# A hybrid SSD and attention layer: the issue orders of the engines rewritten from the state sums to the last output tiles

## The chip, the cores and the metric

One core of a Trainium2 chip runs the whole program. The time is the device time of one execution in microseconds, lower is better. TensorE is called PE, VectorE DVE, ScalarE ACT, GpSimd POOL and SyncE SP, as in the profile.

## The reference

One layer of a streaming encoder, for a prompt of 512 frames and for the next 64 frames of a running stream. D_MODEL is 1024; there are 8 SSD heads of 64 with a state of 128, and 8 latent attention heads.

```python
h = rmsnorm(x, norm_mix); proj = h @ w_in           # z, xbc, dt_raw, cq, ckv_raw
xbc, conv_new = causal_conv(xbc, conv_buf, conv_w, conv_b)   # 4 taps, silu -> xs, B, C
dt = softplus(dt_raw + dt_bias); A = -exp(a_log)
y, h_new = ssd_scan(xs, dt, A, B, C, ssm_h0)        # chunks: per chunk
    # cum = cumsum(dt*A); decay = exp(cum_l - cum_s), causal
    # y = (decay * (C.B) * dt) . x + exp(cum) * (C . h)
    # h = exp(cum_last) * h + (exp(cum_last - cum) * dt * x) . B
y_ssd = rmsnorm((y + d_skip * xs) * silu(z), ssd_norm)
q = rmsnorm(cq) @ w_uq; c_kv = rmsnorm(ckv); q_rope, k_rope rotated
o = mla_attend(...)      # softmax(q.k, block causal) . keys_c, then @ w_uv
x = x + concat(y_ssd, o) @ w_out
hf = rmsnorm(x, norm_ffn)
x = x + (silu(hf @ w_gate) * (hf @ w_up)) @ w_down  # D_FF = 2816
y = rmsnorm(x, norm_final)
```

Outputs are y for both groups, the new latent keys, the new SSD states and the last three convolution rows.

## The kernel before

The 512 + 64 = 576 columns of both groups run together, in two halves of 288. Channels lie on the 128 partitions. Large products keep float32 accuracy by splitting each operand into a high and a low part of type fp32r: `split_weights` (lines 123 to 129) has ACT cast a raw weight tile wr to wh (L127) and DVE subtract to get wl (L128), and each product is three matmuls, wh with x high, wh with x low, wl with x high. `product_halves` (L455) does that for one half of 288 columns in one PSUM bank and then calls an evacuation.

The stages that matter here, in order of time:

- Convolution tiles, `conv_tile` (L394): DVE adds three taps into cacc, ACT takes a tanh, cth (L410), and DVE multiplies into xs (xsd) or into B and C (bc, L412 for the prompt, L413 for the 64 sample columns). Tile 7 is the last of them; its two DVE steps need cth7.
- z tiles, `z_tile` (L471): ps_z on PE, DVE's evacuation into zh (L476), ACT's tanh zt (L479), DVE's product sz.
- SSD by chunks of 128 columns, chunks 0 to 3 for the prompt and chunk 4 for the 64 sample columns. `chunk_a` (L490) has SP load the cumulative sums from DRAM: cumb, and ecp in two halves (L502); PE transposes xs (ps_x) and B (ps_b, L514) and multiplies B with C (ps_b, L515). `chunk_e` (L520) forms the decays E by exponentials on ACT (L529) and the exponential of ecp (L530). `chunk_b` (L543) makes the outputs ps_y and the part from the state, ps_i (L561); `chunk_s` (L565) the state sum ps_s and the new state h. `gate` multiplies with silu(z).
- Attention by head pairs: `pair_proj` (L618) makes ps_q and ps_k, copied to qs and ks; `scores` (L673) makes sc and sc_s (L686), `soft` (L656) takes the max (mx) on DVE, the exponential pr with its sum on ACT (L664), and scales pr by 1/sum on DVE for the first head (L670) and on ACT for the second (L668). `turn` (L692) transposes pr on PE into ptp (L702) and copies it to pt, by ACT for the first head and DVE for the second (L704); `turn_s` is the same for the sample columns (ptp_s, L710). `values` multiplies with V (pv, L727), `values_s` likewise (pvs, L738).
- cat_y: DVE scales xs by the norm factor Ry (L775), ACT casts the high part (L157), DVE subtracts the low part (L159).
- Output projection, `out_tile` (L746): ps_o (L465), added to the residual x2 by DVE (L758); o0 uses the SSD half of w_out and cat_y, o1 the attention half as well.
- Feed-forward, from about 242 us to the end, two thirds of the span.

The code lists the steps in two strings (ORDER_SSD, ORDER_ATT) that fix which instructions exist. The order in which each engine takes its instructions is another matter: at the very end `issue_in_order` reads one table for each engine, ISSUE, a list of positions among the instructions made for that engine, and ties each to the one ahead of it. So each engine's list is fixed by hand, and semaphores only make it wait.

```python
def issue_in_order(tc, nc):
    engines = {"PE": nc.tensor, "DVE": nc.vector, "ACT": nc.scalar, "POOL": nc.gpsimd, "SP": nc.sync}
    info = mybir.DependencyInfo(mybir.DependencyClass.NoSync, mybir.DependencyReason.DATA)
    for name, text in ISSUE.items():
        made = [i for i in nc.cur_bb.bb.instructions if i.engine == engines[name].engine]
        order = list(_places(text))
        for a, b in zip(order, order[1:]):
            tc.add_manual_dep(made[b], made[a].name, info, reason="issue order")
```

A second table, PLACES, fixes the buffer that each temporary, weight tile and PSUM bank takes. It stays.

Of the kernel before, what the change touches and what calls it, by code (L numbers as in the profile page):

```python
# [1319 lines left out]
602-612 637 641-644 638-640 657-659 665-688 660 689-736 661-662 737-760 771-794 663-664 645-652 763-766 653-656  # L1320
795-818 767-770 761-762 819-826 859-861 833-836 862-864 827-832 865-866 837-839 867 880-883 840 868-870 841 845-852
871-873 853-856 874-879 842-843 904-906 857-858 884-887 907-909 844 888 910-912 892-903 889-891 913-915 925-934
916-921 935 939-940 922-924 936-938 949-957 964-965 941 966 945-948 967-969 942-944 970-971 958-963 972-974 976-979
975 987-988 980 984-985 1003 991-993 981-983 986 1015 1004-1006 989 994-995 1016-1021 996 1007-1014 1022-1026
1029-1034 997 1043-1045 990 1000-1002 998-999 1046-1054 1035-1042 1027-1028 1059-1060 1055 1075-1092 1056-1058
1093-1104 1121-1123 1065-1067 1124 1061-1062 1071-1072 1063-1064 1130-1132 1068-1070 1125-1129 1073 1133-1156
1105-1108 1074 1229-1237 1119-1120 1238 1241 1239-1240 1242-1252 1157 1111-1114 1109-1110 1253-1264 1158 1176
1265-1276 1115-1118 1159-1161 1177-1179 1162-1175 1277-1285 1289-1290 1180-1183 1188-1189 1184-1187 1205-1206
1190-1192 1227 1193-1198 1291-1297 1199-1201 1228 1202-1204 1286-1288 1215-1220 1207-1214 1221 1318 1222-1224 1298
1225-1226 1299-1306 1319 1307 1320 1308-1317 1321-1322 1330-1332 1323 1342-1343 1348-1351 1344-1345 1352-1354 1346  # L1330
1355 1347 1333 1324-1329 1334-1341 1356-1363 1368 1364-1366 1369-1370 1367 1371-1393 1404 1394-1396 1405-1406
1397-1403 1407-1415 1428 1416-1427 1429-1433 1440-1441 1434-1435 1442 1436-1439 1572 1443-1447 1452 1448 1453-1456
1449 1457-1458 1450 1459-1460 1451 1461-1462 1587 1578 1584 1463 1581 1573 1464-1478 1579 1479-1486 1575 1488 1487
1489 1585 1490-1497 1500 1498 1501-1503 1499 1586 1588 1504-1506 1576 1574 1507 1580 1508-1509 1512 1577 1513 1510
1514-1515 1511 1516-1517 1605 1518-1522 1593 1523-1525 1582-1583 1526-1527 1606 1528-1531 1602 1536 1532 1537 1533
1538 1534 1603 1539 1607 1535 1589 1540-1541 1599 1542-1544 1594 1608 1545-1550 1600 1551-1552 1595 1614 1553-1555
1609 1560 1556-1557 1626 1561-1565 1615 1558-1559 1566-1568 1616 1569-1570 1604 1571 1596 1590 1597-1598 1601 1591
1610 1617 1620 1623 1621 1635 1627 1622 1592 1636 1629 1637 1628 1611 1641 1618 1630 1624 1631 1612-1613 1625
1658-1659 1642 1644 1650 1660 1647 1661-1662 1632-1633 1663 1651 1648 1664-1665 1619 1656 1638-1640 1666 1643 1667
1634 1668 1645 1669 1646 1649 1652-1654 1657 1694 1670-1672 1695-1697 1673 1682 1698 1655 1674 1699 1675 1700 1718  # L1340
# [12 lines left out]
1988-1989 2042 2013 1990 2043 2055 2006 2056 2014-2015 1991 2007 2001 2044 2048 1992-1993 2057 2002 2058-2059 1984
2008-2009 2045 2016 2003-2005 1985-1986 2017 2049 2046-2047 1994 1987 1995 2010 1996 2011 2018 1997 2060-2061 2019
2062 2020-2021 2030 2063 2022 2031 2064 2023 2065-2066 2050 2067-2069 1998 2032 2070 2051-2052 1999 2053 2033
2071-2073 2034 2074-2075 2084-2086 2076 2078 2035 2077 2079 2036 2087 2080-2081 2037 2088 2082 2114 2083 2102 2090
2089 2038 2091 2103 2039-2040 2115 2092 2041 2093 2104 2094 2105 2095 2106 2096 2107 2116-2118 2138 2097-2099 2139
2108 2100 2109 2101 2119 2110 2192 2111-2112 2120 2113 2121 2126 2122 2127 2123 2128-2130 2140 2131 2144 2132 2145
2193 2133 2124 2134 2146-2148 2135 2149-2150 2136 2194 2137 2141 2125 2142 2195-2196 2151 2143 2197 2156 2152-2153
2157-2158 2154 2159 2168 2160-2162 2180 2155 2163 2181 2169 2164-2165 2182 2174 2222 2170-2171 2216 2166 2210 2175  # L1360
2172 2183 2173 2167 2184 2223 2217 2176 2211 2177 2224 2186 2212 2225 2187-2188 2218 2178-2179 2219 2213-2215 2185
2189-2190 2226 2191 2234 2198 2220 2199-2200 2235 2228-2230 2221 2204 2231-2232 2236 2201 2237-2239 2233 2227
2205-2206 2240 2202 2246 2241 2203 2242 2252 2243-2245 2207 2247 2253-2254 2248 2270 2255 2208 2282 2256-2258 2283
2259-2260 2271-2272 2261 2284 2262-2264 2273 2285 2209 2265 2286 2266 2274 2267 2275 2268 2287 2269 2288-2289 2276
2290 2277 2249 2306 2291-2292 2294 2278 2295 2307 2279 2296 2280-2281 2297-2303 2293 2318-2319 2308 2304 2309-2310
2320 2305 2311 2250 2321-2323 2312-2313 2251 2314 2330 2315-2316 2331 2317 2332-2333 2324 2334-2335 2325-2326 2336
2354 2327 2366-2367 2337 2342 2338 2368-2370 2343 2339-2340 2371 2355 2328 2344-2348 2356 2349 2372 2341 2350-2352
2357 2373-2374 2358 2353 2390 2375 2359-2361 2376 2362-2363 2329 2364-2365 2377-2382 2391-2393 2402-2403 2394
2404-2405 2383-2385 2395 2386 2406 2387 2407 2388-2389 2408 2396-2398 2409 2399-2400 2410 2401 2414-2418 2438 2411
2419-2420 2426-2428 2421 2429 2422 2450 2412 2423-2424 2451 2439 2430-2431 2413 2452 2440 2432 2425 2453 2441-2442  # L1370
2433 2443-2444 2434 2445 2435 2446 2436 2447 2437 2454 2528 2474 2448 2529 2455-2457 2530 2449 2531-2532 2475-2476
2462 2477 2533 2458-2459 2463-2464 2478-2479 2465-2466 2480 2558 2467 2481 2468-2471 2482 2472-2473 2483 2516 2559
2484-2485 2460 2486 2461 2487 2492 2517 2493 2560 2518 2546 2504 2494 2488 2519 2552 2495-2497 2553 2505 2520 2547
2506-2507 2521 2548 2498-2499 2549 2489 2500 2510 2501 2508 2502 2550-2551 2561 2490 2509 2554 2503 2511 2491 2555
2512-2513 2562-2563 2514-2515 2570 2522-2523 2571 2524 2556 2525 2564 2526-2527 2557 2534-2535 2565 2572 2566-2569
2540 2582-2584 2573 2541 2574 2542 2585 2575-2576 2536-2539 2588 2577 2589 2586 2578-2579 2590 2543 2580-2581
2591-2592 2606-2609 2544 2610 2594-2595 2545 2593 2587 2596-2597 2611-2613 2598 2618 2599-2601 2619 2614 2602
2615-2617 2620 2603-2604 2621 2605 2622 2642 2623-2624 2648-2649 2625 2643 2650 2630 2626 2631-2632 2627 2633-2637
# [234 lines left out]
```

## Time and profile before

| | us |
|---|---|
| median of 3 runs | 640.44 (639.99 to 640.5) |
| the profiled execution | 639.58 |
| its span, first to last instruction | 637.5 |
| PE busy | 626.2 (98%) |
| DVE busy | 551.4 (86%) |
| ACT busy | 390.4 (61%) |

The granted clock was 0.998 of full speed. Rows of a timeline give the start, the time from the first start to the last end of a row's instructions (x2, x4: so many together), the engine, the line, the operation, out<-in without buffer numbers, the shape, and in brackets the idle time ahead and what ended it. An f32 matmul counts as two passes in these rows. A PE instruction's end is modelled, so the next start may lie ahead of it, and a short wait can hide below it.

### The profile page before, as it was taken

What the parts mean: (1) busy time and instruction counts of PE and PEld (TensorE: products, weight loads), DVE (VectorE), ACT (ScalarE), POOL (GpSimd) and SP (SyncE); (2) the same over time, 40 slices, a digit from 0 to 9 for tenths busy, and PEclk for the clock granted to TensorE, in tenths of its full rate; (3) what the DMA queues carried; (4) which work ended last, traced back from release to release, by engine and by line L of the source; (5) the groups of instructions that cost most, each with busy time, mean ns of one, the idle gap of its engine ahead of it and who ended that gap; (6) DMA issues with size and microseconds to landing.
All of it is one profiled execution on the core that took longest, in us unless ns stands there. A gap on an engine that the chain in (4) does not pass through costs nothing.

```text
span 637.5 us, 11950 instructions
## 1 busy us (share of the span) xinstructions
PE 626.2 (98%) x4639; PEld 598.0 (94%) x4639; DVE 551.4 (86%) x980; ACT 390.4 (61%) x751; POOL 70.7 (11%) x111
## 2 busy tenths in 40 slices
PE   9999999999999999999999999999999999999994
PEld 9899999985887899999999999999999999999994
DVE  6999996899867599999998997889888998998763
ACT  7655425789766479955656565655565656545463
POOL 1322122001010000000012002100211011100022
PEclk9999999999999999999999999999999999999999
DMA  9522185314131132231187427550765274723004
GB/s 310 207 51 78 35 209 151 114 30 147 72 111 34 62 131 73 93 108 67 36 202 158 128 91 163 141 136 40 189 159 133 67 182 111 181 74 133 1 1 149
DMA packets 31560, 72.66 MB, mean 114 GB/s; under 512 B 3706, under 2 KB 11400, under 8 KB 31248
## 3 DMA queue, kind: packets, MB, share of 16 engines
q1 hardware_dynamic: 25360, 60.77, 29.8%
q0 software_dynamic: 5424, 10.57, 9.3%
q8 instruction: 36, 0.59, 0.4%
q10 hardware_dynamic: 720, 0.57, 0.3%
q14 instruction: 20, 0.16, 0.1%
HBM read 58.03 MB, written 3.30 MB: 96 GB/s over the span
## 4 chain that ended last, share of the span: by engine, by line
PE 48%; issue 1%; DVE 1%; ACT 1%; POOL 1%; POOLq 0%; DVEq 0%
PE ps_x L894 17%; PE ps_dx L1034 9%; PE ps_z L894 9%; PE ps_dz L1034 5%; PE ps_y L894 4%; PE ps_dy L1034 2%; PE ps_l L1104 2%; POOL x L1157 0%; DVE x L1145 0%; DVE sq_last L1194 0%; DVE ss L1192 0%; POOL ss L1238 0%; POOLq L1600 0%; ACT sq L1233 0%; ACT x L1149 0%
## 5 line engine op out<-in xcount | busy, mean ns | idle before, releaser
L894 PE MATMUL ps_x<-xop,wh_gu_S 128*128 128x288 f32 x504 | 126.2, 295 | 0.0
L894 PEld LDWEIGHTS ps_x<-xop,wh_gu_S 128*128 128x128 f32 x504 | 88.2, 188 | 0.7 <-ACT u L963 0.2
L894 PE MATMUL ps_x<-xop,wl_gu_S 128*128 128x288 f32 x252 | 73.2, 295 | 0.0
L894 PE MATMUL ps_z<-xop,gu_a 128*128 128x288 f32 x252 | 61.7, 295 | 0.0
L127 ACT CAST wh_gu_S<-gu 128x1024 fp32r<-128x1024 f32 x44 | 46.2, 1053 | 14.8 <-PE ps_y L894 4.2
L128 DVE TENSOR_TENSOR wl_gu_S<-gu,wh_gu_S 128x1024 fp32r<-128x1024 f32 x44 | 52.8, 1217 | 0.8 <-ACT wh_gu_S L127 0.5
L894 PEld LDWEIGHTS ps_x<-xop,wl_gu_S 128*128 128x128 f32 x252 | 47.1, 188 | 0.0
L1047 POOL DMA_DIRECT2D x<-db x16 | 14.9, 930 | 277.9 <-ACT db L1040 247.8
L143 PE MATMUL ps_in<-xs,wh_in 128*128 128x288 f32 x256 | 45.5, 298 | 0.0
L894 PE MATMUL ps_y<-xop,wh_gu_A 128*128 128x288 f32 x168 | 44.9, 295 | 0.0
L894 PEld LDWEIGHTS ps_z<-xop,gu_a 128*128 128x128 f32 x252 | 43.5, 188 | 0.0
L894 PE MATMUL ps_z<-xop,wh_gu_S 128*128 128x288 f32 x168 | 43.4, 295 | 0.0
L894 PE MATMUL ps_x<-xop,wh_gu_A 128*128 128x288 f32 x168 | 42.7, 295 | 0.0
L143 PEld LDWEIGHTS ps_in<-xs,wh_in 128*128 128x128 f32 x256 | 37.8, 189 | 0.2
L127 ACT CAST wh_gu_A<-gu 128x1024 fp32r<-128x1024 f32 x22 | 23.1, 1051 | 23.0 <-PE ps_x L894 16.1
L894 PEld LDWEIGHTS ps_y<-xop,wh_gu_A 128*128 128x128 f32 x168 | 30.1, 188 | 0.1
L894 PEld LDWEIGHTS ps_z<-xop,wh_gu_S 128*128 128x128 f32 x168 | 29.7, 188 | 0.0
L128 DVE TENSOR_TENSOR wl_gu_A<-gu,wh_gu_A 128x1024 fp32r<-128x1024 f32 x22 | 26.8, 1217 | 3.3 <-ACT wh_gu_A L127 1.8
L894 PEld LDWEIGHTS ps_x<-xop,wh_gu_A 128*128 128x128 f32 x168 | 29.5, 188 | 0.0
L465 PE MATMUL ps_o<-cat_y,wh_out 128*128 128x288 f32 x128 | 29.0, 312 | 0.0
L143 PE MATMUL ps_in<-xs,wl_in 128*128 128x288 f32 x128 | 27.5, 296 | 0.0
L465 PE MATMUL ps_o<-cat_o,wh_out 128*128 128x288 f32 x128 | 27.3, 297 | 0.0
(594 smaller groups left out, 2002.8 us busy)
## 6 DMA issues: line engine op xcount, KB each, us to landing
gu<-in_w_gu SPq DMA_DIRECT2D x44, 512.0 KB, 4.8
db<-in_w_down SPq DMA_DIRECT2D x16, 512.0 KB, 4.5
x<-db POOLq DMA_DIRECT2D x16, 288.0 KB, 6.5
x<-dc POOLq DMA_DIRECT2D x16, 288.0 KB, 4.1
wr_in<-in_w_in SPq DMA_DIRECT2D x8, 512.0 KB, 6.2
wr_out<-in_w_out SPq DMA_DIRECT2D x8, 512.0 KB, 3.3
cumb<-cumD SPq DMA_DIRECT2D x5, 512.0 KB, 5.0
x<-in_xT SPq DMA_DIRECT2D x2, 1152.0 KB, 6.6
```

The lines of the kernel that those rows point to most:

```text
L127: act.copy(hi, raw)
L128: dve.tensor_tensor(lo, raw, hi.bitcast(F32), ALU.subtract)
L143: pe.matmul(ps[:m, hf, :n], w, x[:, hf * n : (hf + 1) * n], start=start and k == 0 and i == 0, stop=stop and k == last and i == 2,)
L465: pe.matmul(ps[:, :n], w, x[:, cols], start=not onto and k == 0 and i == 0, stop=onto or (k == len(terms) - 1 and i == 2), skip_group_chec ...
L894: pe.matmul(ps, p, q, start=not onto and first and kp == kps[0] and j == 0, stop=onto or (last and kp == kps[-1] and j == 2), skip_group_c ...
L1034: pe.matmul(ps, l, r, start=not onto and k == 0 and j == 0, stop=onto or (k == n - 1 and j == 2), skip_group_check=onto,)
L1047: pool.dma_start(x2[t], v, accum_op=ALU.add)
L1104: pe.matmul(ps, w, x[:, cols], start=first and k == 0 and i == 0, stop=last and k == len(terms) - 1 and i == 2,)
```

## The change

Only the ISSUE table differs. All instructions, buffers and step lists are the same. On PE the positions from about 630 to 1500 of 4392 are put in another order (92 to 242 us of the profiled execution of before), on DVE 156 to 411, on ACT 78 to 298, on SP 40 to 65; POOL's list is the same. One line of ACT's table, before and after:

```diff
-47 64 53 37 68 54-55 57-58 72 59 61 38-39 62 76 63 65-66 77 67 69-71 92 73-75 79 78 90 81-82 94 87 80 83 86 104 84
+47 64 53 37 68 54-55 57-58 72 59 61 38-39 62 76 63 65-66 77 67 69-71 92 73-74 89 104 94 79 90 75 84 80 78 81-82 102 98
...
```

What that means on ACT just behind the convolution of tile 7 (a number after a name, as in ecp4, is the chunk or tile; the number after the underscore is a buffer's). Before:

```order
L406 ACTIVATE cacc7_1122<-up7_1114,hcw_502 128x579
L410 ACTIVATE cth7_1127<-cacc7_1122 128x579
L498 ACTIVATE el4_1249<-cumb4_1247 128x8
L479 ACTIVATE zt0_1192<-zh0_1191 128x576
L498 ACTIVATE el0_1307<-cumb0_1305 128x8
L529 ACTIVATE E4_1271<-cumb4_1247,ncum_499 64x64 x2
L127 CAST wh_z1_1390<-wr_z1_1388 128x1024
```

And now, at the same place of ACT's list:

```order
L406 ACTIVATE cacc7_1122<-up7_1114,hcw_502 128x579
L530 ACTIVATE ecp4_1251<-ecp4_1251 128x4x64
L530 ACTIVATE ecp0_1309<-ecp0_1309 128x512
L127 CAST wh_z1_1390<-wr_z1_1388 128x1024
L498 ACTIVATE el4_1249<-cumb4_1247 128x8
L498 ACTIVATE el0_1307<-cumb0_1305 128x8
L410 ACTIVATE cth7_1127<-cacc7_1122 128x579
```

The tanh cth7 moves behind five instructions that were after it, three of which work on data from DMAs. On SP one of the two halves of ecp4 is now issued ahead of wr_z1, so that the second half of ecp0 comes last of the four. On DVE the 512-column product of bc for tile 7 moves up ahead of the evacuations of z.

On PE, where attention begins, the sample scores of the first pair (sc0_s) and the last query projection of the second (ps_q1_1). Before:

```order
L465 MATMUL ps_q1_1_1917<-cqn1_487,wh_pair1_1830 128x288 x2
L465 MATMUL ps_q1_1_1917<-cqn1_487,wl_pair1_1831 128x288
L686 MATMUL sc0_s_2012<-ks0_383,qs0_382 64x320 x2
L680 MATMUL sc1_3_0_2022<-ks1_385,qs1_384 128x512
L702 MATMUL ptp0_0_0_2041<-ident_84,pr_0_0_2004 128x128
L702 MATMUL ptp0_0_0_2041<-ident_84,pr_0_1_1976 128x128
L702 MATMUL ptp0_0_0_2041<-ident_84,pr_0_2_1990 128x128
L702 MATMUL ptp0_0_0_2041<-ident_84,pr_0_3_1950 128x128
L680 MATMUL sc1_3_1_2024<-ks1_385,qs1_384 128x512
L680 MATMUL sc1_2_0_2064<-ks1_385,qs1_384 128x384
```

Now:

```order
L686 MATMUL sc0_s_2012<-ks0_383,qs0_382 64x320 x2
L465 MATMUL ps_q1_1_1917<-cqn1_487,wl_pair1_1831 128x288
L680 MATMUL sc1_3_0_2022<-ks1_385,qs1_384 128x512
L702 MATMUL ptp0_0_0_2041<-ident_84,pr_0_0_2004 128x128
L702 MATMUL ptp0_0_0_2041<-ident_84,pr_0_1_1976 128x128
L702 MATMUL ptp0_0_0_2041<-ident_84,pr_0_2_1990 128x128
L702 MATMUL ptp0_0_0_2041<-ident_84,pr_0_3_1950 128x128
L680 MATMUL sc1_3_1_2024<-ks1_385,qs1_384 128x512
L702 MATMUL ptp0_2_0_2093<-ident_84,pr_0_2_1990 128x128
L702 MATMUL ptp0_2_0_2093<-ident_84,pr_0_3_1950 128x128
L680 MATMUL sc1_2_0_2064<-ks1_385,qs1_384 128x384
```

The sample scores come ahead of the last projection matmul, which makes qs1 for sc1_3_0, and two transposes of the third block come up behind sc1_3_1. Elsewhere PE's list is interleaved more finely: halves of two z tiles alternate, single transposes and the four ps_i4 matmuls of chunk 4 stand between fp32r matmuls of z, and pvs1 stands ahead of and inside pv1. On DVE and ACT at the end of the region the split of w_out's tile out1_0 (wh_out1_0, wl_out1_0) moves about 10 us of work later, and wh_out1_2 moves behind the first feed-forward cast.

More of the change, by code (lines that the diff above doesn't have):

```diff
@@ L1324 @@
[L1324 to L1328, printed above, removed]
@@ new lines @@
+731-733 763 738-739 663 740-741 734 742 735-736 743-750 771 751-754 772 755-757 773-776 768 758-760 777-778 764
+779-781 655 782-791 645-652 792-793 795-796 664 656 797-798 794 765 799-801 766 802-806 769 807-817 833 818 761-762
+819-826 859 837 770 834 862 838 863-864 860-861 839 831 835 827-828 832 836 829-830 865-866 868 840 880-881 867
+869-870 882-883 845-852 871-873 853 841 874 854 884 875 855 876 856 885 877 886 857 878-879 904-905 842 858 843-844
+906 910-912 907-909 887-888 892-901 889-891 902-903 913-915 925-934 916-921 939 935 922-924 940 936-938 949-950
@@ new lines @@
+1142 1145 1105 1146-1147 1143-1144 1148-1153 1106 1229 1154-1156 1230-1234 1108 1235 1241 1109-1110 1107 1157
+1236-1237 1242 1238-1239 1243 1119 1240 1244-1246 1069 1247-1249 1070 1120 1250-1251 1253 1252 1111 1115 1112-1113
+1254 1114 1255 1158 1265 1256 1266-1267 1257 1268-1269 1258 1270-1271 1259 1159-1160 1260-1261 1272-1273 1262 1116
+1274 1263 1275 1117 1264 1118 1176 1277 1161 1179 1278 1177 1279 1276 1178 1170-1172 1162 1173-1175 1163-1169 1180
+1280-1281 1181-1182 1282-1283 1188 1183 1289 1189 1290 1284 1184-1187 1193-1195 1205-1206 1190 1196-1197 1191-1192
@@ new lines @@
+1454-1455 1450 1456-1460 1451 1573 1581 1584 1461-1474 1575 1475-1486 1488 1487 1489 1585 1490-1491 1579 1587
+1492-1497 1500 1498 1501-1503 1499 1586 1588 1504-1506 1576 1574 1507 1580 1508-1509 1512 1577 1513 1510 1514-1515
+1511 1516-1517 1605 1518-1522 1593 1523-1525 1582-1583 1526-1527 1606 1528-1531 1602 1536 1532 1537 1533 1538 1534
+1603 1539 1607 1535 1589 1540-1541 1599 1542-1544 1594 1608 1545-1550 1600 1551-1552 1595 1614 1553-1555 1609 1560
+1556-1557 1626 1561-1565 1615 1558-1559 1566-1568 1616 1569-1570 1604 1571 1596 1590 1597-1598 1601 1591 1610 1617
@@ new lines @@
+1620 1623 1621 1635 1627 1622 1592 1636 1629 1637 1628 1611 1641 1618 1630 1624 1631 1612-1613 1625 1658-1659 1642
+1644 1650 1660 1647 1661-1662 1632-1633 1663 1651 1648 1664-1665 1619 1656 1638-1640 1666 1643 1667 1634 1668 1645
+1669 1646 1649 1652-1654 1657 1694 1670-1672 1695-1697 1673 1682 1698 1655 1674 1699 1675 1700 1718 1683 1719
+1676-1677 1701 1678 1684 1702 1679 1685 1703 1680 1704 1686 1681 1720 1687 1721 1688 1722-1723 1689 1724 1690-1691
+1706 1692-1693 1725 1707 1726 1705 1727-1728 1708-1709 1730 1710-1711 1729 1712 1731-1732 1713-1717 1733-1734
@@ new lines @@
+1824 1828 1825 1829 1854 1830-1831 1855 1832 1856 1886-1887 1833 1857-1860 1888 1834 1889-1890 1861 1891 1835 1892
+1836 1893 1837 1894-1900 1910-1913 1901-1903 1922 1946 1923 1904 1914-1915 1905-1907 1947 1924 1948 1916-1917
+1934-1937 1925 1918-1919 1949 1920 1938 1926-1927 1939-1940 1921 1950 1928 1908 1929 1909 1951 1930 1952 2024 1941
+1970 1931 2025 1971 1932-1933 1942-1944 1953 1972 1945 1954-1956 1958-1959 1973 1960 1974-1975 1961 1976 1962-1963
+1977 1964 2026 1965-1966 2027-2028 1967 1978 1957 2029 1968-1969 2000 1979 2012 1980-1982 2054 1983 1988-1989 2042
@@ new lines @@
+2856-2857 2872 2868 2873-2875 2869 2894-2895 2876 2882-2887 2896-2897 2888 2906 2877 2907 2878 2898-2899 2889 2900
+2879 2890 2880-2881 2908 2901-2903 2891 2904 2892 2905 2909 2893 2910-2915 2930 2916-2921 2942 2922-2923 2931
+2924-2927 2932 2928-2929 2933 2954 2934 2943 2935 2955 2944 2956 2936 2945-2947 2937 2948 2957 2949 2938 2950 2958
+3032 2951-2953 2959 3033 2960 2939 3034 2940 2961 2978-2980 2941 2981 2962-2963 3035 2982 2964 2983-2984 3036
+2966-2967 2985 2968-2971 2986 2972-2976 3037 3020 2965 3008 2987-2988 2977 2989-2990 3021 2991 3009 3022 3056 3014
@@ L1443 @@
+4165 4184 4200 4226 4173 4201 4174-4177 4239 4194 4227 4207-4208 4228-4230 4240-4242 4202 4243 4231 4185 4209 4195
+4262 4210 4186 4232 4211-4212 4263 4233 4213 4234 4214 4235 4244 4264 4203 4215 4223 4217 4204 4220 4245 4236 4218
+4237 4216 4265-4266 4219 4224 4246 4267 4221 4225 4250-4251 4268-4270 4247 4271 4252 4274 4253 4275 4254 4276-4277
+4248 4255 4222 4278-4279 4272 4256 4249 4273 4257-4259 4280 4260-4261 4281-4391
 """,
@@ L1477 @@
+920-921 923 870 922 917 894 918 924-925 916 895 928 902 927 937 926 929 896 938 932 931 939 930 933-934 940 935-936
+941 946 942 944 943 945 947 951 949 948 954 950 952-953 955-979
 """,
@@ new lines @@
+563 568-569 566 564 561 567 565 571 570 572 577 574 576 575 573 578 580 579 589 582 586 588 581 587 592 590 597 585
+583 591 584 594 602-603 595 599 596 600 605 598 601 604 606 610-611 609 608 593 612 607 613 630 614 619 616 625 615
+624 621 617-618 622 626 623 620 627-629 632 631 637 633-636 640 638-639 643 645 648 646 651 654 644 649 647 656 641
+650 657 655 659 658 663 660 642 661 664-665 652 666 662 674 667 669 653 675 670 668 677 676 671-672 686 673 684 680
+678 685 682 681 688-690 679 692 687 693-700 691 701-704 683 705-719
```

314 lines of the change are left out of this document (143 added, 171 removed).

## The prediction

> **What bounds the kernel now.** I read the page's busy line first, then a table of busy time by stretch of the span, then the chain of waits, and last the timelines of the engines around each gap of PE.
>
> ```profile
> PE 626.2 (98%) x4639; PEld 598.0 (94%) x4639; DVE 551.4 (86%) x980; ACT 390.4 (61%) x751; POOL 70.7 (11%) x111
> ```
>
> The table by stretch gives for each the sum, then busy time (and instructions) of PE, PEld, DVE, ACT and POOL, the granted clock, the DMA share and GB/s.
>
> ```profile
> 94.00:134.00 40.00, 40.00 (x313) 36.95 (x313) 30.73 (x61) 25.88 (x70) 7.50 (x9) 1.00 0.38 113
> 134.00:164.00 30.00, 28.75 (x188) 22.05 (x187) 29.22 (x65) 25.61 (x67) 1.96 (x4) 1.00 0.28 88
> 164.00:242.00 78.00, 78.00 (x573) 66.63 (x572) 58.44 (x133) 51.96 (x123) 2.00 (x4) 1.00 0.25 86
> 300.00:600.00 300.00, 299.90 (x2260) 299.23 (x2259) 271.78 (x430) 175.77 (x298) 27.75 (x32) 1.00 0.48 124
> ```
>
> PE is the bound. The feed-forward part (300 to 600) is full and keeps its order, and its rate, 300/2260 = 0.133 us a matmul, is my unit below. The changed orders act between about 92 and 244 us. There PE is visibly idle only between 134 and 164, for 30.00 - 28.75 = 1.25 us, and in that stretch DVE is busy 29.22 of 30. So the only stage with something to win is one where a second engine is full too. PE and DVE there:
>
> ```profile
> 156.14 0.66 PE L702 MATMUL ptp<-ident,pr 128*128 128x128 f32 x4 [0.92 <-DVE pr L670]
> 156.63 2.31 PE L680 MATMUL sc<-ks,qs 100*128 100x512 f32 x6
> 159.27 0.41 PE L710 MATMUL ptp_s<-ident,pr 128*64 128x128 f32 x2 [0.21 <-DVE pr L670]
> ```
>
> ```profile
> 133.89 0.69 DVE L578 TENSOR_TENSOR h<-h,ps_s 128x512 f32<-128x512 f32 x1 [0.49 <-PE ps_s L571]
> ...
> 155.81 0.28 DVE L670 TENSOR_SCALAR pr<-pr,sm 128x128 f32<-128x128 f32 x1
> ...
> 161.26 2.09 DVE L159 TENSOR_TENSOR cat_y<-xsd,cat_y 128x576 fp32r<-128x576 f32 x3
> ```
>
> The long wait is PE's transpose of pr_0_0 at 156.14, 0.92 us for DVE's scaling of pr_0_0, which ends at 155.81 + 0.28 = 156.09. DVE gets there from the state update h_1 at 133.89 almost without a pause, and goes on so until the third cat_y ends at 161.26 + 2.09 = 163.35.
>
> Waits under a neighbour's modelled end show only as a group that takes too long to the next start:
>
> ```profile
> 194.18 0.53 PE L465 MATMUL ps_o<-cat_y,wh_out 128*128 128x288 f32 x2
> 194.54 0.29 PE L465 MATMUL ps_o<-cat_y,wl_out 128*128 128x288 f32 x1
> ...
> 232.08 0.79 PE L465 MATMUL ps_o<-cat_o,wh_out 128*128 128x288 f32 x4
> 232.71 0.42 PE L465 MATMUL ps_o<-cat_o,wl_out 128*128 128x288 f32 x2
> ```
>
> The group at 194.18 takes 0.36 to the next start where two matmuls need 0.27: 0.09 lost, at the least. At 232.08 four take 0.63 where they need 0.53: 0.10. All the waits that an order could take from PE are then 1.25 + 0.09 + 0.10 and a few like these, under 2 us, 0.3% of the span.
>
> **Part 1: the 134 to 164 stretch.** In both orders the same 50 instructions stand on DVE from h_1 to the scaling of pr_0_0, and h_1 waits for the same place of PE's list (ps_s1). From there to the third cat_y the set is the same but for one reciprocal that moves in. So DVE reaches these points when it did, less what of its own idle time goes: 30 - 29.22 = 0.78 us at the most. PE's new order brings sc0_s ahead of the last ps_q1_1 matmul, so sc1_3_0 has to wait longer for the copy of qs1; that lies ahead of the transpose that DVE holds until 156.1, and costs nothing while DVE holds it (up to 0.5 us if DVE came earlier). Behind it, the wait of ptp_s (0.21) goes because pr_0_4 is scaled ahead of a max; but ptp0_2_0 moves up behind sc1_3_1 (at about 157.5), where it needs ACT's copy of ptp0_0_0:
>
> ```profile
> 158.30 0.57 ACT L704 COPY pt<-ptp 128x512 f32<-128x512 f32 x1
> ```
>
> That copy has 1.0 us less of ACT's work ahead of it than before (a scaling, an exponential and cat_y0 go behind it, 1.5, and one scaling, 0.5, comes ahead), so it ends near 157.87: a new wait of about 0.35. Both threads end at cat_y3, 163.35, after which PE has seven matmuls and a transpose to do in place of seven matmuls. I take -0.05 us; bounds -0.78 (all of DVE's idle time) and +0.35.
>
> **Part 2: new waits at 95 us.** ACT's order changes most here.
>
> ```profile
> 93.17 0.69 ACT L410 ACTIVATE cth<-cacc 128x579 f32<-128x579 f32 x1 [5.67 <-DVE cacc L408]
> 93.76 0.20 ACT L498 ACTIVATE el<-cumb 128x8 f32<-128x8 f32 x1
> 97.57 0.69 ACT L479 ACTIVATE zt<-zh 128x576 f32<-128x576 f32 x1 [3.61 <-DVE zh L476]
> 98.16 0.20 ACT L498 ACTIVATE el<-cumb 128x8 f32<-128x8 f32 x1
> 98.27 0.57 ACT L529 ACTIVATE E<-cumb,ncum 64x64 f32<-64x64 f32 x2
> 98.75 1.03 ACT L127 CAST wh_z<-wr_z 128x1024 fp32r<-128x1024 f32 x1
> 99.68 0.34 ACT L529 ACTIVATE E<-cumb,ncum 64x64 f32<-64x64 f32 x1
> 100.68 0.62 ACT L530 ACTIVATE ecp<-ecp 128x512 f32<-128x512 f32 x1
> 101.20 0.58 ACT L529 ACTIVATE E<-cumb,ncum 64x64 f32<-64x64 f32 x2
> ```
>
> The exponentials of ecp4 and ecp0, the cast of wh_z1 and el4, el0 now stand ahead of cth7. They wait for DMAs. Those issues on the SP queue, the landing of the two ecp halves of that moment, and the DVE and PE instructions behind cth7:
>
> ```profile
> 83.28 0.59 SPq L134 DMA_DIRECT2D wr_z<-in_w_in  x1
> 83.91 1.36 SPq L502 DMA_DIRECT2D ecp<-cumD  x2
> ```
>
> ```profile
> DMA to landing us min/median/max: 9.0/9.1/9.3
> ```
>
> ```profile
> 94.79 0.21 DVE L413 SCALAR_TENSOR_TENSOR bc<-cth,cacc 128x64 f32<-128x64 f32 x1
> ```
>
> ```profile
> 95.67 0.33 PE L515 MATMUL ps_b<-bc 128*64 128x64 f32 x2
> ```
>
> The halves issued at 83.9 and 84.6 landed at about 93.2 and 93.6. The same bytes are queued, with ecp4 now ahead of wr_z1 and ecp0 last, so ecp0 is there at about 93.6. From it, start to start: ecp 0.52, wh_z 0.93, el 0.20, el 0.11; cth7 starts at 95.36 instead of 93.17 and ends at 96.05; bc takes 0.21, to 96.26. PE's ps_b stood at 95.67 and has one ps_i4 matmul more ahead of it (two of the eight passes below, 0.20), so it comes at 95.87: a new wait of 0.39 us with nothing over it. Lower bound 0 (landing by 93.2), upper 0.6 (landing 0.2 later: the two halves landed 0.4 apart). ACT's list is strict: the cast of wh_z, whose data had been issued at 83.28, started at 98.75 because zt ahead of it waited 3.61 us for zh. [...] The z tiles behind, now interleaved on PE, need zh from DVE with one half tile's margin; by the same walk along the rows DVE is there 0.3 to 0.9 us ahead, and I cost them at nothing.
>
> **Part 3: interleaving as such.** PE now changes 85 times instead of 45 from plain f32 matmuls to fp32r ones.
>
> ```profile
> 113.38 0.68 PE L550 MATMUL ps_y<-E,xdt 64*64 64x64 f32 x16
> 113.99 0.66 PE L506 MATMUL ps_x<-ident,xsd 128*128 128x128 f32 x4
> 114.48 1.00 PE L561 MATMUL ps_i<-bc,h_s 128*128 128x64 f32 x8
> 115.29 0.52 PE L465 MATMUL ps_z<-xs,wh_z 128*128 128x288 f32 x2
> 115.65 0.29 PE L465 MATMUL ps_z<-xs,wl_z 128*128 128x288 f32 x1
> ```
>
> From 115.29 two fp32r matmuls take 0.36 where they need 0.27, so 0.09 too long. But the eight passes ahead of them take 0.81, 0.10 each, where the four transposes at 113.99 take 0.12 each: at least 0.08 too short. A change costs about 0.01 net, 40 of them 0.4; I take +0.2, with 0 as the other bound. What does cost is another tile size:
>
> ```profile
> 171.41 0.33 PE L738 MATMUL pvs<-pts,V 64*64 64x64 f32 x4
> 171.67 1.12 PE L680 MATMUL sc<-ks,qs 100*128 100x512 f32 x2
> ```
>
> Sixteen passes of 64*64 take 0.61 to the next start, four take 0.26: 0.03 a pass, and 0.14 for going in and out. Both orders have the same runs of small tiles but for one, since pvs1 and pv1 merge. I take -0.15, bounds -0.3 (twice that) and +0.3 (pvs inside pv may disturb it as much). [...]
>
> **Part 4: 164 to 244.** The waits at 194.18 (0.09) and 232.08 (0.10) go, since the copies that they need stand earlier on DVE or the matmul later on PE. After 222.8 DVE is full again with the first feed-forward weights, and the evacuation that PE needs at 234.3 has the same DVE work ahead of it; so of the second wait little need come through. I take -0.15, bounds 0 and -0.5 (a few more like them). Moved weight casts (wh_out1_0, wh_out1_2) fall where ACT has room, 51.96 of 78 busy; without that room each costs 0.95 us.
>
> **Sum.** -0.05 + 0.39 + 0.20 - 0.15 - 0.15 = +0.24 us. The profiled execution took 639.58, its span 637.5 and 2.08 around it; it lies 0.86 below the median, 640.44, of the runs shown. 639.58 + 0.24 + 0.86 = 640.7.
>
> **Rivals.**
> - Faster: DVE's chain from h_1 contracts, so the waits really go. For it: its 0.78 us idle, and each input comes earlier. Against: the same 50 instructions, 97% full. It decides when pr_0_0 is scaled before 155.5. Then -0.78 there and -0.30 for parts 3 and 4, with no wait at 95 and a free alternation: 640.44 - 1.1 = 639.3; with all the waits gone, 2 us, 638.4. I put it at 638.8.
> - Slower: ACT blocked by the ecp landings. For it: 9 us from issue to landing on a full queue. Against: the bytes are the same. It decides from a landing at 93.2; each us later is one us, as PE has no slack up to h_1. Two us more, 95.6, with DVE's zh and PE's ps_z late behind it: 640.44 + 0.39 + 2.0 = 642.8.
> - Slower: the visible long step after each change (115.29 to 115.51 stands inside the 0.52) isn't paid back in a denser interleave: 40 x 0.09 = 3.6, 644.0. Against it is the 0.08 given back ahead of it.
> - The table does not reach the engines as it says: then 640.4, inside the forecast; the new wait at 95 and the place of ptp0_2_0 would tell.
>
> **Numbers.** About 0.2%, 1.3 us, is what a measurement of this kernel tells from no change. Forecast 0.48 (640.7, between 639.2 and 641.7); DVE contracts 0.22; ecp late 0.22; dense interleave 0.04; other new waits among some 900 moved instructions 0.04. Faster 0.22, same 0.48, slower 0.30. The range leaves out 0.1 on each side: 638.6 (the lower part of the first rival) to 642.8.
>
> **What would show it.** Right: the first transpose of pr_0_0 still waits for DVE near 156; cth starts at 95 or later, and PE's ps_b waits for bc just ahead of 96.3; no wait near 194. Wrong: PE busy over 29.7 of 30 between 134 and 164 (DVE was not the bound); ps_z waiting for zh between 96 and 116 (the margins of part 2); or fewer matmuls in 94 to 134 with no named wait (part 3).

## The result, and the profile after

| | before | after |
|---|---|---|
| median of 6 runs beside each other, us | 640.47 (639.78 to 640.84) | 643.53 (641.83 to 646.46) |
| ratio, 95% interval | | 1.0054 (1.0031 to 1.0077) |
| the profiled execution, its span | 639.58, 637.5 | 646.46, 644.6 |
| mean granted clock in it | 0.998 | 0.989 |

The change costs 3.1 us where 0.2 were forecast, and 643.53 lies above the range, which ended at 642.8. The profiled execution is the longest of the six, so what it shows is a bad case; a second profile of the same kernel follows among the experiments (644.04). The page's busy line, and the table by stretch (sum, busy time and count of PE, PEld, DVE, ACT, POOL, then granted clock, DMA share, GB/s):

```profile
PE 629.8 (98%) x4639; PEld 601.7 (93%) x4639; DVE 554.6 (86%) x980; ACT 391.0 (61%) x751; POOL 71.1 (11%) x111
```

```profile
94.00:134.00 40.00, 37.03 (x276) 34.41 (x275) 26.28 (x50) 21.69 (x60) 7.23 (x9) 0.91 0.38 106
134.00:164.00 30.00, 28.02 (x184) 22.35 (x181) 29.08 (x65) 25.68 (x66) 2.48 (x5) 0.98 0.18 57
164.00:242.00 78.00, 77.90 (x557) 65.19 (x556) 58.30 (x131) 51.25 (x124) 1.93 (x4) 0.99 0.26 87
300.00:600.00 300.00, 300.00 (x2265) 299.71 (x2264) 272.98 (x433) 174.17 (x299) 27.75 (x32) 1.00 0.48 127
```

PE does the same work and is busy 3.6 us longer, which no wait explains: the clock column does. Between 94 and 134 us PE gets through 276 instructions instead of 313, stands for 3 us, and the clock is 0.91; in the next two stretches it is 0.98 and 0.99. The feed-forward part runs at its old rate. The waits of PE by what ended them (total, times, longest):

```profile
PE ps_b L515 <- DVE bc L413: 3.0, 1, 3.0
...
PE ptp L702 <- DVE pr L670: 0.7, 1, 0.7
PE sc L680 <- ACT qs L630: 0.5, 1, 0.5
PE sc_s L686 <- ACT pr L664: 0.4, 1, 0.4
```

The wait at ps_b is the one that the prediction named, at 3.0 instead of 0.39 us. The timelines around it, ACT first, then POOL, DVE and PE, and the time from issue to landing of the three ecp halves issued between 81.5 and 84.4 us (the last of them is ecp0's):

```profile
92.10 0.42 ACT L530 ACTIVATE ecp<-ecp 128x256 f32<-128x256 f32 x1 [4.96 <-DMA out_convT<-nconv]
94.98 0.63 ACT L530 ACTIVATE ecp<-ecp 128x512 f32<-128x512 f32 x1 [2.46 <-DMA ecp<-cumD]
95.52 1.03 ACT L127 CAST wh_z<-wr_z 128x1024 fp32r<-128x1024 f32 x1
96.45 0.31 ACT L498 ACTIVATE el<-cumb 128x8 f32<-128x8 f32 x2
96.67 0.67 ACT L410 ACTIVATE cth<-cacc 128x579 f32<-128x579 f32 x1
```

```profile
DMA to landing us min/median/max: 7.2/9.2/10.6
```

```profile
96.73 1.70 POOL L523 TENSOR_SCALAR_AFFINE_SELECT cumb<-cumb 64x512 f32<-64x512 f32 x2 [1.03 <-ACT el L498]
```

```profile
97.37 1.14 DVE L413 SCALAR_TENSOR_TENSOR bc<-cth,cacc 128x64 f32<-128x64 f32 x1 [2.86 <-ACT cth L410]
```

```profile
98.57 0.47 PE L515 MATMUL ps_b<-bc 128*64 128x64 f32 x2 [2.97 <-DVE bc L413]
```

Two things differ from the walk in the prediction. ecp0 landed at 94.96, 1.4 us later than the 93.6 assumed. And bc took 1.14 us instead of 0.21: it began while POOL's two selects on cumb ran (96.73 to 98.43), and it ended at 98.51, right with them. Those selects waited for el here (1.03 us), and the new order puts el directly ahead of cth. Behind the stop stands a third thing, in short windows of the same table:

```profile
95.00:98.00 3.00, 0.59 (x4) 0.30 (x3) 0.63 (x1) 2.69 (x6) 1.97 (x4) 0.97 0.87 231
99.00:100.00 1.00, 1.00 (x6) 0.93 (x6) 0.62 (x2) 0.37 (x1) 0.00 (x0) 0.50 0.20 33
103.00:104.00 1.00, 1.00 (x5) 1.00 (x5) 0.00 (x0) 1.00 (x5) 0.00 (x0) 0.50 0.86 190
105.00:106.00 1.00, 1.00 (x10) 1.00 (x9) 0.00 (x0) 1.00 (x3) 0.00 (x0) 1.00 0.00 0
```

At the end of the stop the granted clock falls to 0.50 and comes back only after 104 us; PE does 5 or 6 instructions in a microsecond instead of 10. Measured at the same place of PE's list, the 600th instruction starts 0.36 us earlier than before and the 700th 5.58 later (109.07 against 103.49): 5.94 us, 2.97 of stop and 2.97 more, which go with the half clock. From there to the 950th nothing is added (5.52): the interleaved z tiles cost nothing, as forecast. The other loss lies where attention begins; PE's waits there, and the clock behind them:

```profile
159.25 0.76 PE L686 MATMUL sc_s<-ks,qs 100*64 100x320 f32 x4 [0.44 <-ACT pr L664]
160.82 1.12 PE L680 MATMUL sc<-ks,qs 100*128 100x512 f32 x2 [0.48 <-ACT qs L630]
162.69 1.11 PE L702 MATMUL ptp<-ident,pr 128*128 128x128 f32 x4 [0.74 <-DVE pr L670]
```

```profile
164.00:165.00 1.00, 1.00 (x2) 0.20 (x1) 1.00 (x4) 1.00 (x3) 0.00 (x0) 0.50 0.91 369
```

Three waits, 1.66 us together, stand where there were two of 0.92 and 0.21, and the clock is at 0.50 behind them for 3.41 us (162.70 to 166.11). The list is 7.63 us late at its 1000th instruction (169.15 against 161.52), 2.1 more than at the 950th, and stays about there: the span is 7.1 longer.

### The profile page after: what moved, and what is told of

It is laid out like the page before. It is cut to its first block, busy times and chain, and to the rows that moved or that the text cites. A ratio compares the mean times of both kernels' runs of the same rounds, so it can differ in the third digit from the quotient of the medians.

```text
span 644.6 us, 11947 instructions
## 1 busy us (share of the span) xinstructions
PE 629.8 (98%) x4639; PEld 601.7 (93%) x4639; DVE 554.6 (86%) x980; ACT 391.0 (61%) x751; POOL 71.1 (11%) x111
## 3 DMA queue, kind: packets, MB, share of 16 engines
HBM read 58.03 MB, written 3.30 MB: 95 GB/s over the span
## 4 chain that ended last, share of the span: by engine, by line
PE 89%; DVE 5%; ACT 2%; issue 2%; POOL 1%; DMA 0%; POOLq 0%; DVEq 0%; ACTq 0%
PE ps_x L894 21%; PE ps_z L894 10%; PE ps_dx L1034 9%; PE ps_o L465 8%; PE ps_in L143 8%; PE ps_y L894 5%; PE ps_dz L1034 4%; PE ps_z L465 3%; PE ps_first L143 2%; PE sc L680 2%; PE ps_dy L1034 2%; PE ps_l L1104 2%; PE ps_p L894 2%; PE ptp L702 2%; PE pv L727 1%
## 5 line engine op out<-in xcount | busy, mean ns | idle before, releaser
L465 PE MATMUL ps_o<-cat_y,wh_out 128*128 128x288 f32 x128 | 31.0, 324 | 0.0
L465 PE MATMUL ps_z<-xs,wh_z 128*128 128x288 f32 x128 | 28.2, 316 | 0.0
```

Of the source, the lines that this page charges most:

```text
L465: pe.matmul(ps[:, :n], w, x[:, cols], start=not onto and k == 0 and i == 0, stop=onto or (k == len(terms) - 1 and i == 2), skip_group_chec ...
```

## The experiments

Three sets, each on one chip beside runs of the kernel before (its medians: 640.45, 639.92 and 640.63). ACT's numbers are 75 cth7, 89 ecp4, 104 ecp0, 94 wh_z1, 79 el4, 90 el0. The theory was that the late cth makes the stop and the stop makes the half clock; the rival, that the finer order of PE costs by itself, as the prediction's third rival had it.

**Cth first.** Only one entry of ACT's list is taken back.

```diff
-... 92 73-74 89 104 94 79 90 75 84 80 ...
+... 92 73-75 89 104 94 79 90 84 80 ...
```

> The changed kernel, with one move taken back: the first threshold exponential cth of the second group stands on ScalarE again right behind its cacc, ahead of the exponentials that read the broadcast cumD (ecp). Theory 1 (the late cth makes PE stand 3.0 us at ps_b, and that stop costs a second time through a granted clock of 0.50 for some 6 us): no wait of PE at ps_b, clock near 1.00 from 94 to 112 us, and about 5.5 us less at 112; the stops near 160 and their half clock may stay. 638.5 to 641. Theory 2 (the finer order of TensorE's own matmuls costs the 3 us): about 643.

(The expectations call cth, a tanh, a threshold exponential.)

Measured: 641.33, ratio 1.0012 (0.9999 to 1.0024). Its table by stretch, and bc, from the shortest of the twelve executions (639.46):

```profile
94.00:112.00 18.00, 18.00 (x140) 17.53 (x140) 11.29 (x21) 10.42 (x29) 4.53 (x7) 1.00 0.55 149
```

```profile
L413 DVE SCALAR_TENSOR_TENSOR bc<-cth,cacc x1: 222/222/222, 94.2 to 94.2; 128x64 f32<-128x64 f32 x1
```

No stop, no half clock, bc back at 0.22 us. PE's finer order is all there, so it isn't the cause of the 3 us. The time is 0.3 above the range that was expected; the three waits stay, near 155 in this profile.

**Cth late in the kernel before.** The same move, made alone in the list of before.

```diff
-... 92 73-75 79 78 90 81-82 94 87 80 83 86 104 84 88-89 85 ...
+... 92 73-74 89 104 94 79 90 75 78 81-82 87 80 83 86 84 88 85 ...
```

> The kernel before, with one move made: on ScalarE alone the two ecp exponentials, wh_z1 and the two el exponentials are put ahead of that cth. Theory 1: PE waits at ps_b for bc by 2 us or more, the clock falls to 0.50 behind it, 643 to 646. If ecp lands at 93.6 here, as in the kernel before, the wait is shorter, and it shows how long a stop the clock bears. Theory 2: 640.5 to 641.

Measured: 642.36 (639.57 to 645.91), ratio 1.0037 (1.0015 to 1.0059). The profiled execution was one of its shorter ones, 640.98:

```profile
96.09 1.72 POOL L523 TENSOR_SCALAR_AFFINE_SELECT cumb<-cumb 64x512 f32<-64x512 f32 x2
```

```profile
95.77 0.23 DVE L413 SCALAR_TENSOR_TENSOR bc<-cth,cacc 128x64 f32<-128x64 f32 x1 [0.87 <-ACT cth L410]
```

```profile
96.05 0.33 PE L515 MATMUL ps_b<-bc 128*64 128x64 f32 x2 [0.29 <-DVE bc L413]
```

Here bc comes 0.3 us ahead of the selects, takes 0.23, and PE waits 0.29: this is the walk of the prediction as it was worked out. The move alone makes the kernel slower on average, but by a different amount in each execution, from 639.57 to 645.91. The expectation's first range was missed at its lower end.

**Cth behind ecp0.** In the changed kernel cth goes ahead of wh_z1 and of both el.

```diff
-... 89 104 94 79 90 75 84 ...
+... 89 104 75 94 79 90 84 ...
```

> The changed kernel, with cth right behind the second ecp exponential, so ahead of wh_z1 and the two el. Theory 1: cth still waits for the landing of ecp, starts near 95.5, bc falls ahead of GpSimd's cumb selects and takes 0.2 instead of 1.1 us; PE waits 0.6 to 1.2 us at ps_b, the clock stays near 1.00, about 641. Theory 2: 643.

Measured: 641.11, ratio 1.0016 (1.0001 to 1.0032), the time as expected. bc is at its old 0.23, a microsecond ahead of the selects, and no wait at ps_b, though ecp0 landed at 94.7 in its profile:

```profile
95.95 0.23 DVE L413 SCALAR_TENSOR_TENSOR bc<-cth,cacc 128x64 f32<-128x64 f32 x1 [0.32 <-ACT cth L410]
```

```profile
97.05 1.70 POOL L523 TENSOR_SCALAR_AFFINE_SELECT cumb<-cumb 64x512 f32<-64x512 f32 x2 [0.23 <-ACT el L498]
```

This profile is one of the longer executions (643.12): at the 600th instruction of PE it was already 0.75 us later than that of before, and the three waits near 156 are followed by half clock (0.86 on average from 158 to 170 us).

**TensorE's list of before, all others changed.** The table of PE is taken from the kernel before, whole.

> The changed kernel with TensorE's list in the order of before; all other lists as changed. Theory 1: the wait at ps_b and the half clock behind it stay, the stops near 160 go back to one of about 1 us without half clock: 641.5 to 643. Theory 2: about 640.5.

Measured: 652.0, ratio 1.0183 (1.0159 to 1.0207), beyond what either theory said. Its longest waits of PE are at other places:

```profile
PE sc L680 <- ACT pr L664: 2.5, 4, 1.1
PE ptp L702 <- DVE pr L670: 1.7, 2, 1.0
PE ps_o L465 <- DVE x L758: 1.6, 1, 1.6
```

Here the list of PE alone, put back, fits the others badly. So it tells nothing on the question; single moves and whole stretches on all engines were used from here.

**The changed kernel once more**, word for word, with a second profile.

> The changed kernel once more, word for word, beside the others of this set and with a second profile. Theory 1 (the price hangs on when ecp lands and on whether the stop of PE halves the clock): the times spread over several us, and those with a lower mean clock are the longer ones; in the profile the start of cth again follows the landing of the second ecp by about 1.7 us, and the stop at ps_b is as long as that landing is late. Theory 2 (a fixed cost of the finer order): the times stand together near 643.5.

Measured: 645.26 (644.04 to 646.76), ratio 1.0079 (1.0062 to 1.0095). The profiled execution took 644.04:

```profile
93.15 0.63 ACT L530 ACTIVATE ecp<-ecp 128x512 f32<-128x512 f32 x1 [1.34 <-DMA ecp<-cumD]
...
94.84 0.67 ACT L410 ACTIVATE cth<-cacc 128x579 f32<-128x579 f32 x1
```

```profile
95.46 1.72 POOL L523 TENSOR_SCALAR_AFFINE_SELECT cumb<-cumb 64x512 f32<-64x512 f32 x2
```

```profile
95.55 1.72 DVE L413 SCALAR_TENSOR_TENSOR bc<-cth,cacc 128x64 f32<-128x64 f32 x1 [1.27 <-ACT cth L410]
```

```profile
97.32 0.33 PE L515 MATMUL ps_b<-bc 128*64 128x64 f32 x2 [1.97 <-DVE bc L413]
```

```profile
98.00:101.00 3.00, 3.00 (x16) 3.00 (x15) 2.33 (x4) 1.83 (x7) 0.00 (x0) 0.51 0.53 71
```

This refutes the half of the theory that the expectation rests on, that the stop is as long as the landing is late. ecp0 landed by 93.15, sooner than the prediction assumed, and cth started at 94.84. With 0.21 for bc PE would have waited 0.46 us. But bc was issued 0.09 us behind the first select and took 1.72, until both were done: 1.5 of the 1.97 us are POOL's. The first select did not wait for el here: it follows POOL's own DMA issues, which end at 95.45, and it starts at 95.46 with cth first too. What el0's new place adds is the second select right behind it, which in the kernel before started only at 98.43. The half clock follows here too, for about 3.4 us (0.54 from 98 to 99, 0.75 from 101 to 102); from the 600th to the 700th instruction of PE the loss is 3.73 us.

**El behind cth.** The last experiment on this place, for that new theory: the changed kernel with the two el, which release POOL's selects, behind cth; cth itself stays behind ecp0 and wh_z1.

```diff
-... 89 104 94 79 90 75 84 ...
+... 89 104 94 75 79 90 84 ...
```

> The changed kernel, with one swap on ScalarE: the two el exponentials, which release GpSimd's cumb selects, stand behind cth instead of ahead of it; cth stays behind both ecp and wh_z1. cth gains only the 0.21 us of el. Theory 1b (the selects hold the 128x64 bc of VectorE up, 1.14 and 1.72 us instead of 0.21, and that is most of the stop): bc takes 0.2 us, the stop at ps_b falls to about 0.4 with an ecp that lands at 93.2 and about 1.4 with one at 95, 641 to 643, and no half clock where ecp lands early. Theory 1a (only the late ecp counts): the stop stays near 2 us or more, 644 to 645.5.

Measured: 642.5, ratio 1.0034 (1.0020 to 1.0049), against 1.0079 (1.0062 to 1.0095) with the two el ahead in the second set and 1.0054 (1.0031 to 1.0077) in the first; the kernel with el ahead did not run beside this one, and the interval of the first set overlaps. In its profile the selects run from 95.46 to 97.18 again, and on DVE and PE stands:

```profile
95.13 0.23 DVE L413 SCALAR_TENSOR_TENSOR bc<-cth,cacc 128x64 f32<-128x64 f32 x1 [0.86 <-ACT cth L410]
...
95.64 2.09 DVE L412 SCALAR_TENSOR_TENSOR bc<-cth,cacc 128x512 f32<-128x512 f32 x1
```

```profile
98.75 0.66 PE L465 MATMUL ps_z<-xs,wh_z 128*128 128x288 f32 x3 [0.71 <-DVE zh L476]
```

bc is 0.4 us sooner, gets ahead of the selects, and the wait at ps_b is gone. Half of the 0.4 is the swap, the other half a landing 0.2 us sooner (ecp0's exponential starts at 92.94 instead of 93.15), so what is shown is what bc ahead of the selects is worth, and not that the swap always brings it there. It is now the next product of the same two operands that runs beside the selects: 2.09 us instead of 0.68, until 97.73, which is 0.55 behind the selects' end. zh stands behind it on DVE and PE's ps_z waits 0.71 for it. The stop of 1.97 has become one of 0.71, and the clock stays at 1.00 in this profile.

**A stop made by hand, and the same stop filled.** Three kernels made from the one before. For the short stop:

```diff
-        act.activation(th, acc, AF.Tanh)
+        for _ in range(6 if t == 7 else 1):
+            act.activation(th, acc, AF.Tanh)
```

> The kernel before with a stop made by hand: the threshold exponential cth of the same tile is computed six times instead of once on ScalarE (the same values into the same tile), so about 3 us later; nothing else differs. bc comes near 97.8 instead of 94.8 and PE stands 2.3 to 2.9 us at ps_b. If only the stop counts: 640.4 + 2.6 = 643.0, clock as before. If a stop of this length also halves the clock for some 6 us: 645 to 646 and a mean clock of 0.993 to 0.994.

For the long one the 6 is a 9:

> The same with cth computed nine times, so about 4.8 us later: PE stands 4.1 to 5.4 us at ps_b. If only the stop counts: 644.5 to 645.8. If the clock halves behind it: 647.5 to 649, clock 0.993 or less.

The filled one has the 9, and in `chunk_a`, ahead of the ps_b product:

```diff
+            for _ in range(16 if (c, g) == (4, 1) else 0):
+                pe.matmul(pb[:L, 256 + P : 256 + P + L], bc[:, 0, tk], bc[:, 2, tk], start=True, stop=True)
```

> The same nine cth, and on TensorE sixteen extra copies of the 128x64 product of the first group ahead of the last ps_b product (into the part of the bank that this one then overwrites), 16 x 0.23 = 3.7 us of work inside the stop. The lateness of bc is the same as in the run without them, but PE works through most of it. If the half clock comes from PE standing still: no half clock behind it, 644.5 to 645.8, some 3 us less than without the copies. If it comes from anything else at that place: the same time as without them, 647.5 to 649.

Measured: 644.25, 646.91 and 645.70; ratios 1.0058 (1.0041 to 1.0075), 1.0106 (1.0088 to 1.0123) and 1.0087 (1.0067 to 1.0106). The stop in each profile, short, long, filled, and a stretch behind it (the added lines of code shift the line numbers a little):

```profile
97.49 0.33 PE L516 MATMUL ps_b<-bc 128*64 128x64 f32 x2 [2.04 <-DVE bc L414]
```

```profile
98.00:101.00 3.00, 3.00 (x26) 3.00 (x24) 1.64 (x3) 1.61 (x5) 0.77 (x2) 1.00 0.05 15
```

```profile
99.35 0.33 PE L516 MATMUL ps_b<-bc 128*64 128x64 f32 x2 [4.17 <-DVE bc L414]
```

```profile
100.00:103.00 3.00, 3.00 (x15) 3.00 (x14) 1.64 (x3) 1.69 (x5) 0.83 (x1) 0.50 0.01 3
```

```profile
99.93 0.33 PE L518 MATMUL ps_b<-bc 128*64 128x64 f32 x2 [2.19 <-DVE bc L414]
```

```profile
100.00:103.00 3.00, 3.00 (x25) 2.93 (x26) 1.89 (x4) 1.17 (x4) 0.77 (x2) 1.00 0.03 8
```

A stop of 4.17 us is followed by 3.4 us of half clock (15 instructions instead of 25 from 100 to 103); with the copies in it the stop is 2.19 and the clock stays at 1.00, though bc is as late. So in these profiles the half clock goes with PE's standing still, and not with the lateness of bc. The copies took 2.1 us, not the 3.7 that I had put down, so more of the stop was left than meant, and in the timed runs the two intervals overlap: the time of this part is not settled by them. The short stop came between its two forecasts, the long one between its own (645.8 and 647.5), the filled one as forecast for a stop without half clock. A stop of 2.04 was borne without half clock, one of 1.97 (the second profile) was not.

**One stretch only, and the rest only.** On all engines the lists of before, but for what stands between 126 and 170 us, in the new order:

> The lists of before on all engines, but for what before issues between 126 and 170 us, which stands in the order of the changed kernel. Theory 1 (this stretch has more waits of PE: qs 0.48, pr 0.73, pr 0.4, cat_y 0.4 against 0.92 and 0.21, so about 1.1 us): 641.0 to 642, and up to 643.5 in executions whose clock halves near 163. The prediction's own figure for it: 640.4.

And the lists of before up to 170 us, the new ones from there:

> The lists of before up to 170 us, those of the changed kernel from there. Theory 1: no wait of PE is added, 0.1 to 0.3 us either way, 640.2 to 640.8, clock as before. Theory 2 (the finer order of TensorE costs): 641.5 or more.

Measured: 641.45, ratio 1.0023 (1.0013 to 1.0033), and 640.79, ratio 1.0001 (0.9991 to 1.0011). Both times are as expected, though not all of the waits. DVE and PE in the first of them, whose profile is its longest execution (643.36):

```profile
133.57 0.69 DVE L578 TENSOR_TENSOR h<-h,ps_s 128x512 f32<-128x512 f32 x1 [0.15 <-PE ps_s L571]
...
149.09 0.17 DVE L665 RECIPROCAL sm<-sm 128x2 f32<-128x2 f32 x1 [0.17 <-ACT pr L664]
...
156.06 0.28 DVE L670 TENSOR_SCALAR pr<-pr,sm 128x128 f32<-128x128 f32 x1
```

```profile
152.97 0.76 PE L686 MATMUL sc_s<-ks,qs 100*64 100x320 f32 x4 [0.44 <-ACT pr L664]
154.54 1.12 PE L680 MATMUL sc<-ks,qs 100*128 100x512 f32 x2 [0.48 <-ACT qs L630]
156.40 1.12 PE L702 MATMUL ptp<-ident,pr 128*128 128x128 f32 x4 [0.73 <-DVE pr L670]
...
171.34 0.87 PE L727 MATMUL pv<-pt,V 128*64 128x384 f32 x4 [0.58 <-ACT pt L704]
```

From h_1 to the scaling of pr_0_0 DVE takes 156.06 - 133.57 = 22.49 us, against 155.81 - 133.89 = 21.92 before. Within that chain there is a wait for ACT now, 0.17; the rest of the 0.57 is in gaps too short to be put down to anything. It is 22.48 or 22.49 in the two profiles of the changed kernel and in those of its three variants on ACT. PE's three waits there add up to 1.65 us against 1.13. The last row is a wait at the seam: neither the kernel before nor the changed one has it, so the 1.0023 contains a wait, 0.58 us in this profile, that the stretch doesn't cost in the changed kernel. The kernel with the rest only has such a wait for pt too, of 0.9 us, where none had been expected.

**The clock in all timed runs.** The mean granted clock of every timed execution is on record. One stretch of 3.4 us at 0.50 takes 0.003 from it (half of 3.41 in 640; in the profiles of the two kernels 0.50 in the last 2.4 and 4.1 us takes a part as well). In the kernel before it is 0.996 to 0.998 in all 65 executions of the three sets.

| kernel | executions at 0.995 or less | their median, us | median of the others |
|---|---|---|---|
| changed, both sets | 8 of 12 | 645.0 | 643.5 |
| before, cth late | 6 of 12 | 644.5 | 641.0 |
| changed, cth behind ecp0 | 5 of 12 | 642.8 | 640.5 |
| changed, cth first | 4 of 12 | 641.7 | 641.2 |
| changed, el behind cth | 2 of 8 | 643.1 | 642.5 |
| stop: short, long, filled | 4 of 6, 4 of 5, 3 of 6 | | |
| stretch from 126 to 170 only | 6 of 12 | 642.4 | 641.2 |
| rest only | 0 of 12 | | 640.8 |

So, taken by the 0.995 of the table, one and the same kernel has the half clock in some executions and not in others; the kernel before (0.996 or more) and the one with the rest only have it in none. The four executions of the changed kernel above 0.995 took 643.3 to 645.3, so most of its 3 us is there without half clock.

## Why the prediction was wrong

- **Part 2** named the right wait at the right place and sized it wrongly. Its walk held from the landing to cth: 1.69 us in the second profile (93.15 to 94.84) where it had 1.76. There 0.46 us would have been left at ps_b if bc had taken 0.21, against the 0.39 of the text, at other absolute times: PE's list lay 0.60 us ahead of that of before. Three steps failed. "bc takes 0.21" was read from a row in which POOL did nothing on cumb; the move of el ahead of cth, seen in the list, was not followed to POOL, whose selects it releases (both in the first profile, the second of them in the second). That is 0.93 us in the first profile and 1.5 in the second. Putting el behind cth lowers the ratio from 1.0079 to 1.0034, some 2.9 us, or 1.3 if the changed kernel's 1.0054 of the first set is taken. "ecp0 is there at about 93.6" held in one profile of two (94.96 in the other, 1.4 us); the bound of 0.2 for it came from two halves of one execution, while in the five profiles in which ACT waited for this half, its exponential started between 92.79 and 94.98. And no clock was costed: it was put at nothing, and the first profile lost 2.97 us behind this stop beyond the stop itself.
- **The rival of a blocked ACT** (642.8) is the nearest to the result, with too small a price: it took one us for each us of landing. In the second profile the landing and the steps from it to cth account for 0.46 of a stop of 1.97 us, in the first for 2.04 of 2.97, so the landing alone doesn't decide it.
- **Part 1** took -0.05, with +0.35 as the upper bound, on the ground that DVE "reaches these points when it did". The same instructions in another order took 0.57 us longer: idle time can grow as well as go, and only its going had been bounded. In the changed kernel DVE is late at h_1 already: 5.97 us behind the kernel before (139.86 against 133.89) where PE's list is 5.52 behind, and it no longer waits for ps_s there. The longer wait of sc1_3_0 for qs1 (0.48) was foreseen and rightly called free on this path: the transposes behind it still wait 0.73 for DVE. With the stretch alone the kernel is 1.5 us (0.8 to 2.1) slower, of which 0.58 is the seam, and the half clock of some executions is part of the rest. DVE as the bound of the stretch was right: 29.08 of 30.
- **Part 3** and the z tiles held: no loss between the 700th and the 950th instruction of PE. **Part 4** held in its sum, 1.0001 (0.9991 to 1.0011) for everything from 170 us on, even with the seam's 0.9 us; but in the second profile PE waits 0.53 us for DVE at 231.12, near the second wait that Part 4 had going.

Of the signs that were named beforehand, these came: cth late (96.67; 94.84 in the second profile, just short of the 95 that was named), a wait of ps_b for bc, a wait of the pr_0_0 transpose for DVE, none near 194, none of ps_z behind the stop. But the wait ended at 98.5 and 97.3 and not ahead of 96.3, and the fall from 313 to 276 instructions between 94 and 134 us had been listed as a sign against part 3; it belongs to the stop and the clock.

The sum in ratios: cth's place explains what lies between 1.0079 (or 1.0054 in the first set) and 1.0012. What is left, 0.8 us by the kernel with cth first, is not clear of zero there (0.9999 to 1.0024); that the stretch from 126 to 170 costs something is shown by the kernel with the stretch alone, with the seam in it.

What stays open: why the times of the changed kernel differ between the two sets (643.5 and 645.3). Part of it stands in the clocks: 3 of 6 executions at 0.995 or less in the first set, 5 of 6 in the second. Open too is when the clock halves behind a stop. The three waits near 160 were followed by half clock in three profiles (from 158 to 170 us 0.86 in the first and in that with cth behind ecp0, 0.93 in that of the stretch alone) and not in three others (1.00 in the second, with cth first, with el behind cth); no experiment varied that alone.

## What to carry to other kernels

When an instruction is moved ahead of a waiting one, follow what it releases on every other engine, and ask which of the released work runs beside the instruction that you have just made late. A duration from the trace holds for the neighbours it had in that trace: bc's 0.21 became 1.14 and 1.72 beside the selects. And a stop of PE had a second price here: behind 1.97, 2.97 and 4.17 us, and behind three waits of 1.66 together, the clock stood at 0.50 for 3.4 us, once for 6.83, and the loss behind the 1.97 had grown to 3.73 by the 700th instruction of PE. Behind 2.04 and 2.19 it did not come, and in the timed runs it came in some executions only; it belongs into the upper bound of any term that adds a wait.

## What the runs showed of the hardware

- DVE's products of cth and cacc, both in SBUF, took longer beside POOL's selects on cumb, in SBUF too: 1.14 and 1.72 us for 0.21, 2.09 for 0.68, ending 0.08, 0.09 and 0.55 us behind the selects. The 1.72 began at 95.55, beside the first select, and ended at 97.27, behind the second (95.46 to 97.18 both). With PE's list of before the 128x512 product took 2.44 though its record begins 0.16 us ahead of the first select (95.71 against 95.87). The product xdt, with one operand in PSUM, took 0.68 beside a select, and 0.68 without one (99.86 in the first profile of the changed kernel). In the kernel before, POOL and DVE:

```profile
96.07 0.68 POOL L523 TENSOR_SCALAR_AFFINE_SELECT cumb<-cumb 64x512 f32<-64x512 f32 x1
```

```profile
96.49 0.68 DVE L508 TENSOR_TENSOR xdt<-ps_x,dt 64x512 f32<-64x512 f32 x1 [1.11 <-PE ps_x L506]
```

- The granted clock fell to 0.50 with stops of 1.97, 2.97 and 4.17 us, and stayed at 1.00 behind stops of 2.04 and 2.19, so in these profiles the length of a stop alone doesn't tell. It stayed at 0.50 for 3.4 us, in the first profile for 6.83. By the clock records the stretches from one change to the next are 27, 2, 17, 1 and 139 times 3.413 us in the first profile (92.16, 6.83, 58.03, 3.41 and 474.45 us) and 184 times in that of the kernel before (628.05). What decides whether the clock falls was not shown.
